# A two-layer block whose second expert layer handles 64 tokens by gathered rows and 192 densely

## The chip, the cores and the metric

The kernel runs on one core of one Trainium2 chip. The metric is the device time of one execution in microseconds (us). Engine names are those of the profile: PE is the matmul engine (TensorE), PEld its weight loads, DVE is VectorE, ACT is ScalarE, POOL is GpSimd, SP is SyncE, which issues most of the DMAs. L1385 is line 1385 of the kernel before.

## The reference

Two layers run over 256 latent tokens `x` and 256 context tokens `ctx`. In each layer a mixer (three kinds of sequence mixing, then an output projection) is followed by a product-key expert layer, `peer_ffn`, for every 128-token block. The change is in that expert layer for the last layer, where only the 256 latent tokens count:

```python
s = einsum('thpd,phkd->thpk', (xb @ w_query), keys)          # 8 heads, 2 halves, 128 keys each
...                                                          # the best 16 of 16*16 sums per head
idx, gate = ...                                              # 8*16 = 128 experts of 16384 for a token
act = gelu(einsum('td,thkd->thk', xb, expert_u[idx]))
out = einsum('thk,thkd->td', gate * act, expert_v[idx])      # expert_u, expert_v: [16384, 1024]
```

So each token uses 128 of the 16384 rows of `expert_u` and of `expert_v`. Everything is float32.

## The kernel before, in words

**Dense and gathered.** `peer` has two ways for a block of 128 tokens. The dense way multiplies the block by all 16384 experts and lets the gates, which are zero but at 128 places, pick. The gathered way fetches for each token (a partition) its own 128 rows of `expert_u` and 128 rows of `expert_v` with indirect DMAs from POOL's queue (`gather`, 128 rows of 4 KB in one DMA) and does the products on DVE: one SCALAR_TENSOR_TENSOR over 128x1024 for each u row (tile `grow`, L1277) and one for each v row (tile `gacc`, L1284). In layer 0 three blocks are dense and one is gathered (`gathered = {0: 0, 1: None}`). In layer 1 both blocks, 256 tokens, are dense.

**A dense expert step.** The 16384 experts go in 128 steps e of 128 experts. U(e) loads a tile of `expert_u` (512 KB, tile `eraw`), splits it into a rounded part `uhi` (ACT, L72) and the rest `ulo` (DVE, L73), multiplies both with the tokens' split `hTh`, `hTl` (the helper `mm3`: hi*hi, hi*lo and lo*hi for each of 8 chunks of the 1024 columns, 24 matmuls of 128 experts by 256 tokens in layer 1), and takes a gelu from PSUM (L1347). V(e) loads a tile of `expert_v`, splits it likewise into `vhi` and `vlo`, multiplies the step's activations by the gates (L1370), splits the product into the two halves of `whl` (L1372, L1373) and accumulates into PSUM (L1385): for each of two token blocks hi*hi, hi*lo and lo*hi over two halves of 512 columns, 12 matmuls of 512 columns. Each pair of split tiles has two buffers, `eraw` has five.

**The stages of layer 1.** After the queries and the top-k search, `gates` writes the dense gates out of one-hot products (L1225 to L1241, blocks of 8 tokens) to memory (`gd`), while U runs ahead for `LEAD[1]` = 56 steps. Of these activations some stay in SBUF and `SPILL[1]` = 14 go to memory and come back (tiles `aout`, `ain`). Then the main loop runs V(e), at first alone; from e = 52 on V(e) is followed by U(e+4). The gates come back in pieces for four steps (`gt`). At the end the residual, the norm and the output are done on DVE and ACT (L1458 to L1482).

**What sets the order.** The queue of each engine is in program order, fixed when the kernel is built by a scheduler with its own clock, so an instruction that waits holds up all behind it on its engine. `side()` puts pieces of the gathered way between the dense steps, `RATE` of them at each call; in layer 1 it has none to put.

## Time and profile before

| | us |
|---|---|
| median of 3 runs (2705.26 to 2716.01) | 2710.6 |
| the profiled execution's own time | 2711.68 |
| its span, first to last instruction | 2709.9 |
| layer 1: U alone beside the gates | about 1944 to 2122 |
| layer 1: V alone | 2122 to 2272 |
| layer 1: V and U in turn | 2272 to 2680 |
| the last V steps and the output | 2680 to 2710 |

The stages are read from the times of the first and last matmuls of each kind. PE is busy 96% of the span, DVE 75%. A busy PE here is one with a matmul in flight; matmuls overlap, so the time from the start of one to the start of the next, not the length of one, is what one costs.

### The profile page before, as it was taken

The numbers are of one execution on the slowest core, as the hardware profiler recorded it, in microseconds if no ns is written. First come the engines' busy times: TensorE is split into PE (matmuls) and PEld (weight loads), VectorE is DVE, ScalarE is ACT, GpSimd is POOL, SyncE is SP. The second block draws the span as 40 slices with busy tenths as digits, with TensorE's granted clock in tenths as the row PEclk, the third lists the DMA queues.
The fourth block names the chain that finished last, engine by engine and source line by source line (L and its number), as shares of the span: only waits on it lengthen the run. The fifth ranks groups of instructions, "written<-read, shape, count | busy, mean of one in ns | idle before, by whom it ended". The sixth has DMA issues, their size and how long they took to land.

```text
span 2709.9 us, 44308 instructions
## 1 busy us (share of the span) xinstructions
PE 2609.6 (96%) x16959; PEld 2264.6 (84%) x16959; DVE 2039.1 (75%) x4344; ACT 1187.5 (44%) x1808; POOL 415.2 (15%) x342
## 2 busy tenths in 40 slices
PE   7899999999899999999999999999899999999998
PEld 4677888898678899898899987868799878999997
DVE  8755589899789988888988855657999666555554
ACT  3343343466334333333333334444467545444443
POOL 0001000011014434344443300010010000000000
PEclk8998999999899999999999999989899999999999
DMA  7521523577679899999999938444577877666663
GB/s 275 129 92 56 176 90 109 192 286 293 224 253 361 316 347 327 344 337 334 326 340 339 339 113 266 136 142 178 175 262 265 280 236 244 209 209 209 208 209 115
DMA packets 253317, 632.77 MB, mean 234 GB/s; under 512 B 25840, under 2 KB 120880, under 8 KB 250288
## 3 DMA queue, kind: packets, MB, share of 16 engines
q1 hardware_dynamic: 198048, 433.19, 46.8%
q0 software_dynamic: 36864, 134.23, 13.7%
q10 hardware_dynamic: 18192, 62.50, 6.4%
q8 instruction: 133, 2.18, 0.3%
q14 instruction: 80, 0.66, 0.1%
HBM read 567.36 MB, written 61.45 MB: 232 GB/s over the span
## 4 chain that ended last, share of the span: by engine, by line
PE 78%; DVE 11%; issue 6%; DMA 3%; ACT 1%; POOL 0%; SPq 0%; DVEq 0%; POOLq 0%; ACTq 0%
PE pu L78 32%; PE acc L1385 28%; PE prT L280 5%; PE prN L294 3%; PE opp L947 2%; PE gps L1238 1%; PE gps L1239 1%; DVE wlo L73 1%; PE modp L158 1%; DMA ain<-act 1%; PE yp L639 1%; DVE ulo L73 1%; DMA mraw<-in_w_mod_dram 1%; DVE s L1096 1%; DVE ti L1095 1%
## 5 line engine op out<-in xcount | busy, mean ns | idle before, releaser
L1385 PE MATMUL acc<-vhi,whl 128*128 128x512 f32 x2528 | 726.2, 397 | 2.0 <-ACT whl L1372 2.0
L78 PE MATMUL pu<-hTh,uhi 128*128 128x384 f32 (+1 forms) x2048 | 605.2, 313 | 11.6 <-ACT s L1182 7.0
L78 PE MATMUL pu<-hTl,uhi 128*128 128x384 f32 (+1 forms) x2048 | 603.8, 313 | 0.0
L1385 PEld LDWEIGHTS acc<-vhi,whl 128*128 128x128 f32 x2528 | 471.4, 189 | 106.8 <-ACT whl L1372 2.3
L73 DVE TENSOR_TENSOR vlo<-eraw,vhi 128x1024 fp32r<-128x1024 f32 x253 | 309.2, 1222 | 261.7 <-ACT vhi L72 259.2
L72 ACT CAST vhi<-eraw 128x1024 fp32r<-128x1024 f32 x253 | 266.1, 1052 | 518.9 <-PE acc L1385 503.4
L1385 PE MATMUL acc<-vlo,whl 128*128 128x512 f32 x1264 | 402.2, 399 | 14.4 <-DVE vlo L73 14.4
L78 PEld LDWEIGHTS pu<-hTh,uhi 128*128 128x128 f32 x2048 | 391.6, 191 | 22.9 <-ACT s L1182 7.2
L78 PEld LDWEIGHTS pu<-hTl,uhi 128*128 128x128 f32 x2048 | 391.9, 191 | 6.8
L72 ACT CAST uhi<-eraw 128x1024 fp32r<-128x1024 f32 x259 | 272.3, 1052 | 269.7 <-PE pu L78 249.3
L73 DVE TENSOR_TENSOR ulo<-eraw,uhi 128x1024 fp32r<-128x1024 f32 x259 | 316.6, 1222 | 87.2 <-ACT uhi L72 66.1
L78 PE MATMUL pu<-hTh,ulo 128*128 128x384 f32 (+1 forms) x2048 | 352.5, 311 | 0.0
L78 PEld LDWEIGHTS pu<-hTh,ulo 128*128 128x128 f32 x2048 | 313.4, 190 | 3.1 <-DVE bsel L1154 0.8
L1385 PEld LDWEIGHTS acc<-vlo,whl 128*128 128x128 f32 x1264 | 238.4, 189 | 72.8 <-DVE vlo L73 16.6
L1271 POOL DMA_INDIRECT grow<-in_v_dram,gidx x128 | 167.9, 1311 | 253.7 <-DVE gacc L1284 196.4
L1271 POOL DMA_INDIRECT grow<-in_un_dram,gidx x128 | 154.5, 1207 | 279.1 <-DVE grow L1277 148.7
L73 DVE TENSOR_TENSOR wlo<-raw,whi 128x1024 fp32r<-128x1024 f32 x84 | 102.1, 1217 | 112.1 <-ACT whi L72 102.8
L1284 DVE SCALAR_TENSOR_TENSOR gacc<-grow,gact,gacc 128x1024 f32<-128x1024 f32 x127 | 162.6, 1280 | 3.0 <-DMA grow<-in_v_dram,gidx 3.0
L1277 DVE SCALAR_TENSOR_TENSOR grow<-grow,h2n 128x1024 f32<-128x1024 f32 x128 | 155.9, 1219 | 8.4 <-DMA grow<-in_un_dram,gidx 8.4
L280 PE MATMUL prT<-hTh,whi 128*128 128x512 f32 (+1 forms) x464 | 158.6, 347 | 2.9 <-ACT whi L72 2.9
L280 PE MATMUL prT<-hTl,whi 128*128 128x512 f32 (+1 forms) x464 | 159.6, 346 | 0.0
L280 PE MATMUL prT<-hTh,wlo 128*128 128x512 f32 (+1 forms) x464 | 157.5, 344 | 1.3 <-DVE wlo L73 1.3
(419 smaller groups left out, 3715.7 us busy)
## 6 DMA issues: line engine op xcount, KB each, us to landing
eraw<-in_ut_dram SPq DMA_DIRECT2D x256, 512.0 KB, 4.3
eraw<-in_v_dram SPq DMA_DIRECT2D x256, 512.0 KB, 4.5
gd<-gst ACTq DMA_DIRECT2D x20, 2048.0 KB, 8.5
mraw<-in_w_mod_dram SPq DMA_DIRECT2D x64, 512.0 KB, 4.8
gt<-gd SPq DMA_DIRECT2D x31, 768.0 KB, 10.4
raw<-in_w_in_dram SPq DMA_DIRECT2D x36, 512.0 KB, 5.0
raw<-in_w_query_dram SPq DMA_DIRECT2D x32, 512.0 KB, 3.8
eraw<-in_w_mod_dram SPq DMA_DIRECT2D x32, 512.0 KB, 6.3
```

The lines of the kernel that those rows point to most:

```text
L72: (hi_eng or nc.scalar.copy)(hi, src)
L73: self.last_lo = (lo_eng or nc.vector).tensor_tensor(lo, src, hi.bitcast(F32), op=OP.subtract)
L78: self.nc.tensor.matmul(out, a, b, start=n == 0, stop=n == len(ops) - 1)
L158: self.nc.tensor.matmul(acc[32 * kc:32 * kc + 32, :], self.sc[:, 4 * half + kc, :], raw[:, o:o + 512], start=half == 0 or not whole, stop= ...
L280: self.nc.tensor.matmul(bs[g][:, pt * n:pt * n + n], a[:, k, gs], b, start=z == 0 and k == 0 and q == 0, stop=z == 1 and k == 3 and q == 2)
L294: self.nc.tensor.matmul(o, a, b[:, k], start=z == 0 and k == 0 and q == 0, stop=z == 1 and k == 3 and q == 2)
L639: nc.tensor.matmul(bb[odd][:, gg, :], hin[hf, z, d, g // 2, :], rhs, start=n == 0, stop=False)
L947: mm = nc.tensor.matmul(ob[64 * k:64 * k + 64, cs], a, r, start=z == 0, stop=z == len(ops) - 1, tile_position=tp)
L1271: nc.gpsimd.indirect_dma_start(out=r, out_offset=None, in_=src, in_offset=bass.IndirectOffsetOnAxis(ap=idx[:, j:j + 1], axis=0))
L1277: v.scalar_tensor_tensor(r, r, 1.0, self.h2n, op0=OP.mult, op1=OP.mult, accum_out=act[:, j:j + 1])
L1284: v.scalar_tensor_tensor(acc, r, act[:, j:j + 1], acc, op0=OP.mult, op1=OP.add)
L1385: nc.tensor.matmul(acc[b][h], w[:, wk, bs], r[:, 512 * h:512 * h + 512], start=e_ == 0 and z == 0, stop=e_ == NI1 - 1 and z == 2)
```

## The change

In layer 1 the first 192 tokens stay dense and the last 64 (the second half of block 3) are gathered. So that the gathered half fills 128 partitions, each token takes two partitions with 64 of its 128 experts each: `h2n`, `gidx` and `ggate` hold tokens 64 to 127 of the block on the upper partitions and a copy for the other 64 experts on the lower ones. There are 64 u gathers and 64 v gathers of 512 KB each. `gates` makes 6 groups of 32 tokens, not 8.

U(e) keeps `hTh` and `hTl` in one tile `hTb`, so that one matmul of 384 columns multiplies `uhi` with both; a matmul of 192 columns multiplies `ulo` with the high part. That is 16 matmuls where there were 24. The two sums lie side by side in PSUM; ACT copies one, DVE adds the other (192 columns), ACT takes the gelu. V(e) writes the low and the high part of the last 64 tokens' activations side by side as one 128-wide stationary operand, so that block costs 4 matmuls of 512 columns and the other still 6: 10 where there were 12. At the end a matmul with a folding matrix adds the two halves of the gathered sums and of that block's PSUM.

`LEAD[1]` goes from 56 to 64, `SPILL[1]` from 14 to 32, and `RATE` for layer 1 is 1.0.

```diff
-LEAD = {0: 40, 1: 56}
+LEAD = {0: 40, 1: 64}
-SPILL = {0: 22, 1: 14}
+SPILL = {0: 22, 1: 32}
-RATE = 2.4
+RATE = {0: 2.4, 1: 1.0}
...
+    def split_tile(self):
+
+        self.hTb = self.hp.tile([128, 2, 8, 512], F32R, name="hTb", bufs=1)
+        return self.hTb[:, 0], self.hTb[:, 1]
...
+            if nat == self.half[l]:
+                nc.scalar.dma_start(self.h2n[0:64], self.h2n[64:128])
...
+        groups = [(b, tg) for b in blocks for tg in range(2 if b == self.half[l] else 4)]
...
+                    nc.vector.tensor_copy(self.gidx[hi], idx[hi, 0:64])
+                    nc.vector.tensor_copy(self.ggate[hi], w[hi, 2, 0:64])
+                    nc.scalar.dma_start(self.gidx[lo], idx[hi, 64:128])
+                    nc.scalar.dma_start(self.ggate[lo], w[hi, 2, 64:128])
...
+                    pu = pu_.tile([128, 2, nt], F32, name="pu", bufs=8 - 2 * nb)
+                    for c in range(8):
+                        cs = slice(c * 128, (c + 1) * 128)
+                        both = lambda: nc.tensor.matmul(pu, hi[:, cs], self.hTb[:, :, c, c0:c0 + nt],
+                                                        start=c == 0, stop=c == 7)
+                        if c < 7:
+                            both()
+                        nc.tensor.matmul(pu[:, 0], lo[:, cs], hs(hh, c), start=False, stop=False)
+                        if c == 7:
+                            both()
...
+                    nc.scalar.copy(acts[e], pu[:, 1])
+                    nc.vector.tensor_tensor(acts[e], acts[e], pu[:, 0], op=OP.add)
+                    nc.scalar.activation(acts[e], acts[e], AF.Gelu_apprx_tanh)
...
+                if half is not None:
+                    nc.scalar.copy(w[:, 2 * nt:], a[:, nt - nt % 128:])
...
-                for b in range(nb):
+                for b in range(nb) if half is None else (1, 0):
...
+                            if 128 * b + 128 > nt:
+
+                                ops = [(w[:, 2 * nt - 64:], r) for r in (hi, lo)]
+                            else:
+                                ops = [(w[:, o:o + 128], r) for o, r in ((128 * b, hi), (128 * b, lo), (nt + 128 * b, hi))]
...
+                    nc.tensor.matmul(b[0:64], fold, t, start=True, stop=True)
+                    nc.tensor.matmul(b[64:128], fold, self.gacc[:, 512 * h:512 * h + 512], start=True, stop=True,
+                                     tile_position=(0, 64))
...
             self.gathered = {0: 0, 1: None}
+            self.half = {0: None, 1: 3}
```

Line numbers in the rows of the changed program are its own (L1376 and L1380 are the two kinds of U matmuls, L1399 the addition, L1306 and L1313 the gathered products, L1423 and L1427 the gate product and the low half of `whl`).

PE in the main loop of layer 1, at the end of one U step and the start of the V step behind it, in the program before:

```order
L78 MATMUL pu<-hTh,uhi 128x256
L78 MATMUL pu<-hTl,uhi 128x256
L78 MATMUL pu<-hTh,ulo 128x256 x8
L1385 MATMUL acc_19974<-vhi,whl 128x512
L1385 MATMUL acc_19975<-vhi,whl 128x512
L1385 MATMUL acc_19974<-vlo,whl 128x512
L1385 MATMUL acc_19975<-vlo,whl 128x512
```

The same place in the changed program:

```order
L1376 MATMUL pu<-hTb,uhi 128x384
L1380 MATMUL pu<-hTb,ulo 128x192 x2
L1376 MATMUL pu<-hTb,uhi 128x384
L1445 MATMUL acc_19772<-vhi,whl 128x512
L1445 MATMUL acc_19773<-vhi,whl 128x512
L1445 MATMUL acc_19772<-vlo,whl 128x512
L1445 MATMUL acc_19773<-vlo,whl 128x512
L1445 MATMUL acc_19770<-vhi,whl 128x512
```

The `ulo` products, which stood in one run of 8 at the end of U, now alternate with the wide ones, and the second token block (`acc_19772`, `acc_19773`) has four matmuls and stands first.

DVE in the same loop, before (one U and two V steps in part):

```order
L73 TENSOR_TENSOR ulo<-eraw,uhi 128x1024
L1370 TENSOR_TENSOR act<-act,gt 128x256
L73 TENSOR_TENSOR vlo<-eraw,vhi 128x1024
L1373 TENSOR_TENSOR whl<-act,whl 128x256
L73 TENSOR_TENSOR ulo<-eraw,uhi 128x1024
```

DVE there in the changed program:

```order
L73 TENSOR_TENSOR vlo<-eraw,vhi 128x1024
L1306 SCALAR_TENSOR_TENSOR grow,gact<-grow,h2n 128x1024
L1313 SCALAR_TENSOR_TENSOR gacc<-grow,gact,gacc 128x1024
L1399 TENSOR_TENSOR act<-act,pu 128x192
L73 TENSOR_TENSOR ulo<-eraw,uhi 128x1024
L1423 TENSOR_TENSOR act<-act,gt 128x192
L73 TENSOR_TENSOR vlo<-eraw,vhi 128x1024
L1306 SCALAR_TENSOR_TENSOR grow,gact<-grow,h2n 128x1024
L1427 TENSOR_TENSOR whl<-act,whl 128x192
```

Gathered products stand between the splits of the dense steps, and each U brings an addition from PSUM.

DVE at the end of the gates of layer 1 (the one-hot products `oh1h`, `oh1l`), before:

```order
L1232 TENSOR_TENSOR oh1h<-oh1l,sel_18998 128x1024
L1233 TENSOR_TENSOR oh1l<-oh1l,sel_18998 128x1024
L73 TENSOR_TENSOR ulo<-eraw,uhi 128x1024
L1233 TENSOR_TENSOR oh1l<-oh1l,sel_18998 128x1024
L73 TENSOR_TENSOR ulo<-eraw,uhi 128x1024
L73 TENSOR_TENSOR vlo<-eraw,vhi 128x1024 x2
L73 TENSOR_TENSOR ulo<-eraw,uhi 128x1024
```

and in the changed program:

```order
L1252 TENSOR_TENSOR oh1h<-oh1l,sel_19032 128x1024
L73 TENSOR_TENSOR ulo<-eraw,uhi 128x1024
L1253 TENSOR_TENSOR oh1l<-oh1l,sel_19032 128x1024
L1399 TENSOR_TENSOR act<-act,pu 128x192
L73 TENSOR_TENSOR ulo<-eraw,uhi 128x1024
L1399 TENSOR_TENSOR act<-act,pu 128x192
L73 TENSOR_TENSOR ulo<-eraw,uhi 128x1024
L1399 TENSOR_TENSOR act<-act,pu 128x192
L1423 TENSOR_TENSOR act<-act,gt_19044 128x192 x2
```

After the last `oh1h`, 3 `ulo` splits stood before the main loop's run of V; now 16 do.

## Rows read from the trace of the kernel before

**Rows 1.** The page: span, then busy us (share of the span) xinstructions.
```profile
span 2709.9 us, 44308 instructions
PE 2609.6 (96%) x16959; PEld 2264.6 (84%) x16959; DVE 2039.1 (75%) x4344; ACT 1187.5 (44%) x1808; POOL 415.2 (15%) x342
```

**Rows 2.** Busy time by stage: us, each engine's busy us, PEclk, DMA share, GB/s.
```profile
core 0: us, PE busy (x) PEld busy (x) DVE busy (x) ACT busy (x) POOL busy (x), PEclk, DMA share, GB/s
1944.00:2122.00 178.00, 176.31 (x1686) 170.58 (x1687) 164.11 (x289) 121.06 (x188) 14.27 (x8) 0.99 0.72 258
2122.00:2272.00 150.00, 146.23 (x629) 117.21 (x628) 95.85 (x154) 69.96 (x105) 0.00 (x0) 0.99 0.75 251
2272.00:2680.00 408.00, 408.00 (x2577) 368.32 (x2577) 227.79 (x294) 195.57 (x290) 0.00 (x0) 1.00 0.62 209
```

**Rows 3.** Chain of waits, main loop of layer 1: start us, us, what.
```profile
2344.51 2.80 PE acc L1385 x12
2347.31 2.87 PE pu L78 x24
```

**Rows 4.** Waits of 1950 to 2710: us in total, times, longest us.
```profile
ACT vhi L72 <- PE acc L1385: 248.2, 122, 2.9
```

**Rows 5.** Timeline of PE, layer 0, one U step: start us, us, operation.
```profile
1243.38 0.33 PE L78 MATMUL pu<-hTh,uhi 128*128 128x384 f32 x1
...
1246.18 1.55 PE L78 MATMUL pu<-hTh,ulo 128*128 128x384 f32 x8
```

**Rows 6.** Timeline of PE, plain float32 matmuls, 128 and 512 columns.
```profile
1864.85 0.60 PE L1180 MATMUL sp<-keys,qTq 128*128 128x128 f32 x4
...
193.84 3.59 PE L664 MATMUL zp<-gyT,wglu 128*128 128x512 f32 x8
```

**Rows 7.** Timeline of DVE, layer 1, V alone.
```profile
2133.03 0.42 DVE L1373 TENSOR_TENSOR whl<-actr,whl 128x256 fp32r<-128x256 f32 x1
2133.37 0.42 DVE L1370 TENSOR_TENSOR actr<-actr,gt 128x256 f32<-128x256 f32 x1
```

**Rows 8.** Timeline of DVE, layer 0, with gathered products.
```profile
1357.72 1.22 DVE L1277 SCALAR_TENSOR_TENSOR grow<-grow,h2n 128x1024 f32<-128x1024 f32 x1
...
1358.87 1.28 DVE L1284 SCALAR_TENSOR_TENSOR gacc<-grow,gact,gacc 128x1024 f32<-128x1024 f32 x1
1360.07 1.22 DVE L73 TENSOR_TENSOR ulo<-eraw,uhi 128x1024 fp32r<-128x1024 f32 x1
1361.20 0.55 DVE L1370 TENSOR_TENSOR act<-act,gt 128x384 f32<-128x384 f32 x1
1361.67 0.42 DVE L364 TENSOR_TENSOR Rst<-rt 128x256 f32<-128x256 f32 x1
```

**Rows 9.** Busy time in two stretches of layer 0 that gather; columns of Rows 2.
```profile
820.00:870.00 50.00, 50.00 (x221) 40.97 (x220) 44.89 (x83) 20.12 (x27) 20.98 (x17) 1.00 1.05 383
1300.00:1400.00 100.00, 100.00 (x502) 90.24 (x501) 92.26 (x190) 36.50 (x48) 47.06 (x35) 1.00 0.97 342
```

**Rows 10.** Groups of DVE, 1944 to 2122: busy us, mean ns | idle.
```profile
L73 DVE TENSOR_TENSOR ulo<-eraw,uhi 128x1024 fp32r<-128x1024 f32 x47 | 57.5, 1223 | 9.5 <-ACT uhi L72 8.1 <-issue 1.1
L1232 DVE TENSOR_TENSOR oh1h<-oh1l,sel 128x1024 f16<-128x1024 f16 x32 | 22.0, 688 | 0.0
...
L1230 DVE TENSOR_SCALAR oh2s<-oh 128x1024 f16<-128x1024 f16 x16 | 6.7, 418 | 0.0
```

**Rows 11.** Groups of ACT, 2400 to 2500.
```profile
L72 ACT CAST uhi<-eraw 128x1024 fp32r<-128x1024 f32 x18 | 19.0, 1053 | 9.9 <-PE pu L78 9.9
...
L1347 ACT ACTIVATE act<-pu 128x256 f32<-128x256 f32 x18 | 6.9, 386 | 0.0
```

**Rows 12.** What ended idle time before the tile ain (us, times), whole run.
```profile
  DMA ain<-act: 16.5, 13
```

**Rows 13.** Busy time in 10 us among those waits; columns of Rows 2.
```profile
2180.00:2190.00 10.00, 8.62 (x30) 6.92 (x31) 6.90 (x11) 3.11 (x5) 0.00 (x0) 0.83 0.71 215
```

**Rows 14.** Timeline of DVE, the output behind the last matmul.
```profile
2696.87 1.89 DVE L1458 TENSOR_TENSOR et<-acc,gaterow 128x512 f32<-128x512 f32 x3 [5.09 <-PE acc L1385]
```

More of the change, by code (lines that the diff above doesn't have):

```diff
@@ L221, in norm_T @@
         s0 = 0 if which == 0 else 3
[L222 to L223 removed]
+        hT = self.split_tile()
         pairs = sorted({b // 2 for b in blocks})
@@ L1051, in mixer @@
             self.selp = self.es_sel.enter_context(self.pool(f"sel{l}", side="right"))
-            if self.gathered[l] is not None:
+            nat = self.gathered[l] if self.half[l] is None else self.half[l]
+            if nat is not None:
                 self.h2n = self.selp.tile([128, 1024], F32, name="h2n")
@@ L1080, in mixer @@
                 self.show("x1", xs[2])
-                self.norm_T(l, 1, xs, blocks, rp, nat=self.gathered[l], stats=ss, apart=blocks)
+                self.norm_T(l, 1, xs, blocks, rp, nat=nat, stats=ss, apart=blocks)
             self.tvp = self.es_tv.enter_context(self.pool(f"tv{l}", side="right"))
@@ L1210, in gates @@
         self.es_tv.close()
-        self.gt0 = es.enter_context(self.pool(f"gt0_{l}", side="right")).tile([128, 4 * len(blocks), HOLD[l], 32], F32, name="gt0")
+        self.gt0 = es.enter_context(self.pool(f"gt0_{l}", side="right")).tile([128, len(groups), HOLD[l], 32], F32, name="gt0")
         with self.pool(f"gate{l}", side="right") as p:
-            for k, b in enumerate(blocks):
+            for gi, (b, tg) in enumerate(groups):
                 sel = sels[b]
-                for tg in range(4):
+                if True:
                     st = p.tile([128, NI1, 32], F32, name="gst", bufs=2)
@@ L1284, in v_item @@
                 v.scalar_tensor_tensor(acc, r, act[:, j:j + 1], acc, op0=OP.mult, op1=OP.add)
-        for h in range(9):
+        for h in range(n // 16 + 1):
             for k in range(16):
-                if h < 8:
+                if h < n // 16:
                     u_item(16 * h + k)
@@ L1301, in peer @@
         nb = len(dense)
-        nt = 128 * nb
+        half = self.half[l]
+        nt = 128 * nb - (64 if half is not None else 0)
+        ng = nt // 32
         c0 = 128 * dense[0]
@@ L1312, in peer @@
             per, away = 1024 // nt, {}
+            kept = 4 * per if half is None else 8
+            held = lead - KEEP - spill - (kept if half is None else 0)
             pu_ = es.enter_context(self.pool(f"psu{l}", space=PSUM))
@@ L1332, in U @@
                 self.u_lo = self.last_lo
-                pu = pu_.tile([128, nt], F32, name="pu", bufs=8 - 2 * nb)
                 hs = lambda t, c: t[:, c, c0:c0 + nt]
-                self.mm3(pu, [((hi[:, c * 128:(c + 1) * 128], lo[:, c * 128:(c + 1) * 128]), (hs(hh, c), hs(hl, c)))
-                              for c in range(8)])
-                if e < 4 * per:
+                if half is None:
+                    pu = pu_.tile([128, nt], F32, name="pu", bufs=8 - 2 * nb)
+                    self.mm3(pu, [((hi[:, c * 128:(c + 1) * 128], lo[:, c * 128:(c + 1) * 128]), (hs(hh, c), hs(hl, c)))
+                                  for c in range(8)])
+                else:
[9 more added lines that the diff above has]
+                            both()
+                if e < kept and half is not None:
+                    acts[e] = acts_b.tile([128, nt], F32, name="act", bufs=held)
+                elif e < kept:
                     if e % per == 0:
@@ L1449, in peer @@
                 out[gb] = (self.gacc[:, 0:512], self.gacc[:, 512:1024])
-            for k, b in enumerate(sorted(out)):
+            if half is not None:
+                out[half] = []
+                fold = ep.tile([128, 64], F32, name="fold", bufs=1)
+                nc.vector.tensor_tensor(fold, self.ident[:, 0:64], self.ident[:, 64:128], op=OP.add)
+                for h in range(2):
+                    t = ep.tile([128, 512], F32, name="ft", bufs=2)
+                    nc.scalar.copy(t, acc[nb - 1][h])
+                    b = pubank([128, 512], "fold")
+                    nc.tensor.matmul(b[0:64], fold, t, start=True, stop=True)
+                    nc.tensor.matmul(b[64:128], fold, self.gacc[:, 512 * h:512 * h + 512], start=True, stop=True,
+                                     tile_position=(0, 64))
+                    out[half].append(b)
+            for k, b in enumerate(sorted(out) if half is None else (3, 2)):
                 ty = b // 2
```

62 lines of the change are left out of this document (38 added, 24 removed).

## The prediction, made before the changed kernel had run

> **What bounds the kernel now.** I read the page first: PE has a matmul in flight for 96% of the span, DVE works 75% [rows 1]. That share is a mean over stages, so next the busy times by stage of layer 1, the only part that the change touches. While U runs beside the gates, PE is busy 176 of 178 us and DVE 164; with V alone 146 of 150 against 96; with V and U in turn 408 of 408 against 228 [rows 2]. So in the last two stages, 558 us, PE sets the pace and DVE is idle two fifths of the time; in the first both are nearly full. The chain of waits agrees: in the main loop it is nothing but V of 12 matmuls for 2.80 us and U of 24 for 2.87 us by turns [rows 3], and the cast of `vhi` waits 248 us in all for PE to give its buffer back [rows 4]. The transfers run at 209 to 258 GB/s there [rows 2]. The change takes work from PE and gives work to DVE and the DMA engines, so the question is which of these two takes PE's place.
>
> **What PE saves.** A V of 10 matmuls costs 10/12 of 2.80 = 2.33 us. A U has 8 wide and 8 narrow ones. Wide: sixteen matmuls of 384 columns in layer 0 take 1246.18 - 1243.38 = 2.80 us, 0.175 each [rows 5]. Narrow (192 columns, this number type): no row. By columns it is 0.175/2 = 0.088. But each brings its own 128x128 weights; four plain float32 matmuls of 128 columns with such weights take 0.60 us, at most 0.15 each [rows 6], and 256 columns cost 2.87/24 = 0.12 now [rows 3]. I take 0.115, near the last, and keep 0.088 to 0.15. Then U = 8 x (0.175 + 0.115) = 2.32 us. PE saves 128 x 0.55 + 128 x 0.47 = 130 us in all.
>
> **What DVE gets.** Durations overlap by 0.08 us, so I use starts: 1.13 to 1.14 us for a split, 0.34 for 256 columns, 0.47 for 384 [rows 7, 8], hence 0.275 for 192. A gathered u product costs 1.15 us, a v product 1.20 [rows 8]. So V = 1.14 + 2 x 0.275 = 1.69 us and U, with its new addition, 1.415. That addition reads PSUM, which these rows do not show for this shape; 0.2 to 0.5 us holds it, and I take the SBUF price.
>
> The order of the built program cuts the loop in three. A: 64 V, 3 U and 60 gathered products (38 u, 22 v). B: 44 V, 45 U and 68 products (26 u, 42 v). C: the last 20 V and 16 U, with none.
> - A: PE 64 x 2.33 + 3 x 2.32 = 156 us. DVE 108.2 + 4.2 + 43.7 + 26.4 = 182 us.
> - B: PE 207 us. DVE 74.4 + 63.7 + 29.9 + 50.4 = 218 us.
> - C: PE 16 x 4.65 + 4 x 2.33 = 84 us, DVE 57.
>
> **What the DMA engines get.** A step's tile and a gather are 512 KB (0.524 MB) each, gates 0.39 MB for four steps, a spilled activation 0.1 MB. A moves 64 + 3 + 60 tiles, 14 gate pieces and 32 returning activations, 75 MB; B 44 + 45 + 68 tiles and 11 pieces, 87 MB. The best long stretch with gathers carried 383 GB/s, with PE never idle; a typical one 342, also with PE never idle, so 342 is a demand and not a limit [rows 9]. At 383 A takes 197 us and B 226, both a little over DVE and well over PE. So in A and B the feed decides, by transfers or by DVE, which lie within 15 us of each other. In A 32 activations come back from memory, where 14 did. Of 36 such tiles in the whole run 13 were waited for, 16.5 us in all [rows 12]: 32 x 13/36 x 1.27 = 15 us, of which I count half, since transfers go on meanwhile. A = 205, B = 229, C = 84: 518 us, against 2697 - 2122 = 575 now [rows 2, 14]. That is -57.
>
> At this place a page speaks against the change. The Trainium skill, DMA: Bandwidth & Descriptors, section Specifications, gives an HBM limit of about 358 GB/s for a core. By it A and B take 162/0.358 = 452 us instead of 434 and the sum ends 18 us later. Row and page differ: 383 over 50 us here, with one core at work.
>
> **Before the loop.** DVE comes to the last gate block earlier: 48 splits with an addition, 67.9 us, stand ahead of it instead of 53 without, 60.4; eight gate blocks fewer, each four one-hot operations of 0.61 and half of one of 0.34 (durations less the overlap of 0.08) [rows 10], 2.6 us, save 21; the extra rows and indices (`h2n`, `gidx`) cost some 3.5. Together -10 us. But 16 U steps stand behind that block where 3 stood, PE's 37.1 us instead of 8.6: +28.5. So V starts 18 us later, with 64 U done and not 56. Bounds -10 (PE finds room for them beside the gates) and +28.
>
> **Smaller edits.** ACT gets a PSUM copy in each U and a 64-column copy in each V, at most 0.39 us each beside casts of 1.05 [rows 11]; it is idle half of the main loop [rows 2], and that hides them; without that cover they would cost up to 0.8 us a step. Three small DMAs on ACT's queue and 18 more spills stand beside the gates, where transfers have room. On POOL four gathers stand ahead of the copies of the first gates, which wait for the last gate group anyway. On SP's queue the 32 returns stand among the loads of V; that wait is counted. One tile `hTb` for two means that a rewrite waits for readers of both; they end together, 0 to 2 us. Layer 0 keeps its work, some reordered: within 5 us. At the end two folds, four plain float32 matmuls of 512 columns at up to 0.45 us a record [rows 6], partly side by side, take the place of waiting for PE [rows 14]: +2.
>
> **The sum.** 2711.7 (the profiled execution's own time, 1.1 above the median of the runs) - 57 + 18 + 2 = 2675 us, or 2674 against the median. About 0.5% is what a measurement can tell from no change: 2697 to 2724.
>
> **Rivals.**
> - *All of PE's saving comes through.* 2711.7 - 130 = 2582. It needs A and B at PE's 363 us, but DVE alone has 400 there. Only a later, denser use of stage C could give it. 0.07.
> - *The feed is slower (the other side).* DVE's queue is in order: when a gathered row is late, the split behind it waits, and PE with it. If the mix of two queues yields R GB/s, A and B take 162/R. At 342, the typical row, the time is 2711.7 + 474 + 84 - 575 + 20 = 2715, no change; that is the point from which it decides (below 335 it is slower by over 0.5%). At 320 it is 2711.7 + 506 + 84 - 575 + 20 = 2747. For it: the small slack in A, where V's two buffers, casts and splits must fit in 2.33 us and a 1.2 us product may stand in between. Against it: 383 in a stretch where DVE did the same mix. Within 0.5% 0.10, slower 0.13.
> - *The clock falls in A.* Where V had waited for returning activations the granted clock was 0.83 over 10 us [rows 13], part of that at the lower level, 1.2 GHz; in steady V and U it was 1.00 [rows 2]. PE would be busy 156 of 205 us in A. At 1.2 GHz a V costs 10 x 512/1.2 = 4.27 us, A 275 us, the whole 2745. Against it: once PE is the slower one it is busy all the time, so this mends itself. Same 0.03, slower 0.04.
> - *The narrow matmuls run at the plain float32 price.* Such a matmul leaves two records of 3.59/8 = 0.45 us for 512 columns [rows 6], so 0.34 us for 192. U = 4.1 us, more than the 2.87 of now: the lead grows by 64 x 4.1 - 56 x 2.87 = 101 us (less some 6 of gate matmuls), B to 287, C to 112: 2711.7 + 95 + 605 - 575 + 2 = 2839. Against it: 256, 384 and 512 columns all cost 0.46 ns a column, with no sign of a step. 0.07.
> - *U does not get cheaper.* At 0.18 us for a narrow matmul U stays at 2.87 and only V saves; C costs 93 and the 16 late U steps 46, the time is 2675 + 9 + 9 + some 5 in B = 2698. Within 0.5% 0.04.
>
> **How the numbers follow.** The forecast, 2635 to 2697, has 0.52. Faster by over 0.5%: 0.52 + 0.07 = 0.59. Within: 0.10 + 0.03 + 0.04 = 0.17. Slower: 0.13 + 0.04 + 0.07 = 0.24. The range goes from 2625 (V starting early and the feed at PE's pace in half of A and B) to 2750 (a feed of 320); it leaves out the plain price, the full saving and some 0.05 of the slower feed, 0.19 in all.
>
> **What would show it.** In the changed profile: narrow matmuls 0.09 to 0.15 us apart; V at 3.1 to 3.3 us a step while alone and V with U at about 5.2 while gathers last; there PE busy about 80 to 90%, DVE over 90%, 370 to 390 GB/s; after the last gather 4.65 us a step with PE full; the first V near 2140 instead of 2122. I am wrong if DVE waits for `grow` by tens of us, if the granted clock in A is below 0.95, or if the stage before the first V is longer by more than 30 us.

## The result, and the profile after

The changed kernel takes 2684.5 us (median of 4 runs, 2681.19 to 2692.46) against 2712.4 (median of 4, 2705.26 to 2716.01): a ratio of 0.990, 95% interval 0.9886 to 0.9915, so 28 us or 1% faster, twice what a measurement can tell from no change. The prediction was 2674, range 2625 to 2750, with the forecast (faster, gathering stages set by the feed) as the likeliest case. The profiled execution took 2692.5, the slowest of its four, so single stages below may be some us long; that of before took 2711.7.

The page answers to [rows 1]: PE has 84 us less, DVE 146 us more.

```profile
span 2689.2 us, 42483 instructions
PE 2525.4 (94%) x15591; PEld 2141.6 (80%) x15591; DVE 2185.1 (81%) x4639; ACT 1217.7 (45%) x2054; POOL 593.8 (22%) x468
```

Busy time by stage, the columns of [rows 2]. The second to fourth rows are the prediction's A, B and C: they end where the low split of the 65th V, that of the 109th V and the last V matmul stand.

```profile
1944.00:2138.00 194.00, 168.01 (x1295) 151.13 (x1294) 171.34 (x355) 128.57 (x241) 19.66 (x10) 0.97 0.77 265
2138.00:2359.00 221.00, 186.34 (x751) 138.16 (x751) 190.68 (x306) 104.33 (x216) 88.25 (x61) 0.96 0.97 348
2359.00:2585.00 226.00, 210.93 (x1123) 177.78 (x1124) 216.76 (x312) 132.21 (x264) 101.17 (x63) 1.00 0.99 375
2585.00:2673.00 88.00, 88.00 (x493) 78.82 (x492) 59.74 (x89) 54.01 (x110) 0.00 (x0) 1.00 0.67 210
```

From first to last V matmul it is 535 us, where it was 572: -37. (The first V matmul of the kernel before stands at 2124.88 and the last at 2697.1; the 2122 and the 575 that the prediction used go by a boundary between stages.) The first V matmul stands 14 us later, the end behind the last V is 3 us longer. Together that makes the 20.7 us by which the span is shorter.

In B, 226 us, nothing is idle for long: the DMA engines are busy 0.99 of the time, DVE 217 us, PE 211. In C only PE is full. In A, 221 us, PE and DVE are each idle for over 30 us although the transfers, at 348 GB/s, are below B's 375. That stage is the odd one. Near its start the chain of waits (start us, us, what) names the tile that comes back from memory in two long pieces:

```profile
2166.56 6.66 DMA ain<-act
2185.05 9.47 DMA ain<-act
```

The DMA issues of the whole run (KB each, median us from issue to landing) show that such a tile takes longer: 5.6 us, where the larger one before took 3.9. First the changed kernel, then the one before:

```profile
ain<-act SPq DMA_DIRECT2D x32, 96.0 KB, 5.6
```

```profile
ain<-act SPq DMA_DIRECT2D x14, 128.0 KB, 3.9
```

DVE itself waited little for it (8.5 us in all, against 16.5 [rows 12]). The wait shows on ACT and PE instead: in the groups of 2165 to 2280, the PE matmuls of the first kind were held 22.9 us, most of it by the cast of `whl`, which stands behind the gate product on the returned tile.

```profile
L1445 PE MATMUL acc<-vhi,whl 128*128 128x512 f32 x191 | 63.3, 434 | 22.9 <-ACT whl L1426 19.6 <-DVE whl L1427 3.0 <-DVE gact L1326 0.2
L1426 ACT CAST whl<-ain 128x192 fp32r<-128x192 f32 x30 | 10.5, 349 | 22.8 <-DVE ain L1423 18.3 <-issue 4.5
L1423 DVE TENSOR_TENSOR ain<-ain,gt 128x192 f32<-128x192 f32 x29 | 9.9, 355 | 4.1 <-DMA ain<-act 4.1
```

But late tiles are not what makes this stage slow. Each gate product can be set beside the landing of the tile that it reads. For the 12th to the 19th V it starts within 0.5 us of the landing, so there the tile does come at the last moment; the low splits of these V go at 3.03 us a step. For the 20th to the 40th V the tile has landed 1.5 to 5.8 us before its product, and the steps from the 19th to the 41st take 3.77 us. These two stretches, in the columns of [rows 2]:

```profile
2173.60:2194.80 21.20, 16.24 (x65) 11.30 (x63) 18.42 (x32) 9.94 (x19) 9.78 (x6) 1.00 1.02 374
2200.20:2276.10 75.90, 58.26 (x207) 40.22 (x206) 58.63 (x92) 29.55 (x61) 24.72 (x20) 0.93 0.94 322
```

In the second, DVE never waits before the gate product (group of 2200 to 2276):

```profile
L1423 DVE TENSOR_TENSOR ain<-ain,gt 128x192 f32<-128x192 f32 x20 | 6.8, 354 | 0.0
```

What holds PE there is the order of the queues. In 18 of the 32 steps with a returned activation the gate product stands on DVE behind the same V's low split. In 12 of them, 11 behind the 19th V, the cast of `whl` also stands on ACT behind the cast of `vhi` for the next V, and its low half on DVE behind the next V's low split. The kernel before has none of either kind. `vhi` has two buffers, so the next V's cast waits until PE is through with the V before; PE then stands idle until both casts are done. At the start of the 34th V (timelines of PE and ACT, put in order of time; the engine's idle time before a row, and what ended it, in brackets):

```profile
2253.59 0.63 PE L1445 MATMUL acc<-vhi,whl 128*128 128x512 f32 x2
2254.30 1.04 ACT L72 CAST vhi<-eraw 128x1024 fp32r<-128x1024 f32 x1 [1.61 <-PE acc L1445]
2255.25 0.35 ACT L1426 CAST whl<-ain 128x192 fp32r<-128x192 f32 x1
2255.65 0.73 PE L1445 MATMUL acc<-vhi,whl 128*128 128x512 f32 x2 [1.43 <-ACT whl L1426]
```

PE's price is read in stage C (timeline of PE), in answer to [rows 3, 5]: U runs from 2600.13 to 2602.42, 2.29 us, V from there to 2604.75, 2.33 us. A wide and a narrow matmul together take 0.285 us: 0.18 to 0.20 to the next start behind a wide one, 0.085 to 0.09 behind a narrow one.

```profile
2600.13 0.34 PE L1376 MATMUL pu<-hTb,uhi 128*128 128x384 f32 x1
2600.31 0.25 PE L1380 MATMUL pu<-hTb,ulo 128*128 128x192 f32 x1
2600.40 0.36 PE L1376 MATMUL pu<-hTb,uhi 128*128 128x384 f32 x1
2600.60 0.25 PE L1380 MATMUL pu<-hTb,ulo 128*128 128x192 f32 x1
...
2602.42 0.63 PE L1445 MATMUL acc<-vhi,whl 128*128 128x512 f32 x2
...
2604.75 0.34 PE L1376 MATMUL pu<-hTb,uhi 128*128 128x384 f32 x1
```

DVE's prices in B (timeline of DVE), in answer to [rows 8]: the addition out of PSUM 0.26 us from start to start, a u product 1.15, a v product 1.19, the gate product 0.27.

```profile
2381.95 0.35 DVE L1399 TENSOR_TENSOR act<-act,pu 128x192 f32<-128x192 f32 x1
2382.21 1.22 DVE L1306 SCALAR_TENSOR_TENSOR grow<-grow,h2n 128x1024 f32<-128x1024 f32 x1
2383.36 0.08 DVE L1306 DVE_READ_ACCUMULATOR grow<-grow,h2n 128x1 f32 x1
2383.36 1.28 DVE L1313 SCALAR_TENSOR_TENSOR gacc<-grow,gact,gacc 128x1024 f32<-128x1024 f32 x1
2384.55 0.35 DVE L1423 TENSOR_TENSOR act<-act,gt 128x192 f32<-128x192 f32 x1
2384.82 1.22 DVE L73 TENSOR_TENSOR vlo<-eraw,vhi 128x1024 fp32r<-128x1024 f32 x1
```

Two questions remain: whether the feed in B is the transfers or DVE, and what holds A. All ratios below are to the kernel before, on the same chip; the changed kernel's is 0.990, and 0.001 is 2.7 us. Paces are from the start of one low split of V to that of the next, "V alone" those of the 9th to the 41st V (the ones with a returned activation), "V with U" those of the 61st to the 109th, "the steps behind" those of the 109th to the 125th.

### The profile page after: what moved, and what is told of

It reads as the page before. It is cut to its first block, busy times and chain, and to the rows that moved or that the text cites. A ratio compares the mean times of both kernels' runs of the same rounds, so it can differ in the third digit from the quotient of the medians.

```text
span 2689.2 us, 42483 instructions
## 1 busy us (share of the span) xinstructions
PE 2525.4 (94%) x15591; PEld 2141.6 (80%) x15591; DVE 2185.1 (81%) x4639; ACT 1217.7 (45%) x2054; POOL 593.8 (22%) x468
## 4 chain that ended last, share of the span: by engine, by line
PE 41%; issue 12%; DVE 10%; DMA 6%; ACT 4%; ACTq 0%; POOL 0%; SPq 0%; DVEq 0%; POOLq 0%
PE acc L1445 20%; PE pu L78 14%; PE pu L1376 2%; DMA act<-aout 2%; DVE ulo L73 2%; DVE vlo L73 2%; PE pu L1380 1%; ACT uhi L72 1%; DVE grow L1306 1%; DMA ain<-act 1%; ACT vhi L72 1%; PE prT L286 1%; DVE wlo L73 1%; DMA raw<-in_w_in_dram 1%; DVE gacc L1313 1%
## 5 line engine op out<-in xcount | busy, mean ns | idle before, releaser
L78 PE MATMUL pu<-hTb,uhi 128*128 128x384 f32 x2048 | 390.9, 341 | 7.7 <-ACT uhi L72 3.8
L1300 POOL DMA_INDIRECT grow<-in_un_dram,gidx x192 | 243.9, 1270 | 603.3 <-DVE grow L1306 198.6
L78 PEld LDWEIGHTS pu<-hTb,uhi 128*128 128x128 f32 x2048 | 362.2, 190 | 17.3 <-ACT actr L1396 4.7
L1300 POOL DMA_INDIRECT grow<-in_v_dram,gidx x192 | 271.2, 1412 | 347.1 <-DVE gacc L1313 215.9
L1376 PE MATMUL pu<-hTb,uhi 128*128 128x384 f32 x1024 | 320.7, 369 | 18.0 <-ACT uhi L72 16.0
L1380 PE MATMUL pu<-hTb,ulo 128*128 128x192 f32 x1024 | 250.2, 265 | 25.7 <-DVE ulo L73 24.8
L1313 DVE SCALAR_TENSOR_TENSOR gacc<-grow,gact,gacc 128x1024 f32<-128x1024 f32 x190 | 243.9, 1284 | 1.8 <-DMA grow<-in_v_dram,gidx 1.7
L286 PE MATMUL prT<-hTb,whi 128*128 128x512 f32 (+1 forms) x928 | 240.2, 346 | 3.5 <-ACT whi L72 3.2
L1306 DVE SCALAR_TENSOR_TENSOR grow<-grow,h2n 128x1024 f32<-128x1024 f32 x192 | 234.4, 1221 | 8.8 <-DMA grow<-in_un_dram,gidx 8.8
L1380 PEld LDWEIGHTS pu<-hTb,ulo 128*128 128x128 f32 x1024 | 198.6, 196 | 48.5 <-DVE ulo L73 41.4
L1376 PEld LDWEIGHTS pu<-hTb,uhi 128*128 128x128 f32 x1024 | 195.1, 193 | 27.6 <-ACT uhi L72 22.6
L78 PE MATMUL pu<-hTb,ulo 128*128 128x384 f32 x1024 | 204.0, 337 | 0.5 <-DVE ulo L73 0.5
L286 PEld LDWEIGHTS prT<-hTb,whi 128*128 128x128 f32 x928 | 159.8, 190 | 31.3 <-ACT whi L72 3.4
```

What stands on the lines that cost most here:

```text
L78: self.nc.tensor.matmul(out, a, b, start=n == 0, stop=n == len(ops) - 1)
L286: self.nc.tensor.matmul(bs[g][:, pt * n:pt * n + n], a[:, k, gs], b, start=z == 0 and k == 0 and q == 0, stop=z == 1 and k == 3 and q == 2)
L1300: nc.gpsimd.indirect_dma_start(out=r, out_offset=None, in_=src, in_offset=bass.IndirectOffsetOnAxis(ap=idx[:, j:j + 1], axis=0))
L1306: v.scalar_tensor_tensor(r, r, 1.0, self.h2n, op0=OP.mult, op1=OP.mult, accum_out=act[:, j:j + 1])
L1313: v.scalar_tensor_tensor(acc, r, act[:, j:j + 1], acc, op0=OP.mult, op1=OP.add)
L1376: both = lambda: nc.tensor.matmul(pu, hi[:, cs], self.hTb[:, :, c, c0:c0 + nt], start=c == 0, stop=c == 7)
```

## Experiments on the stages that gather

**No gathers.** Edit:

```diff
+        if n == 64:
+            v.memset(acc, 0.0)
+            return
         for h in range(n // 16 + 1):
```

> The 128 gathers and their 128 products on DVE are left out, so the last 64 tokens get no expert sum; all else is as in the changed kernel (2684 us). Theory F (in the stages that gather, the feed of transfers and DVE sets the pace): there V and U fall to PE's own 2.33 and 2.29 us, so about 2684 - (218 - 160) - (229 - 206) = 2600 us, and V alone takes 2.3 to 2.6 us a step. Rival A (the activations that come back from memory, tile ain, hold V while it is alone): V alone stays above 3.2 us a step and only the stage of V with U gains, 2655 to 2662. Rival C (PE's clock): the stretch of V alone still shows a granted clock under 0.95.

Measured 2616.8 us, ratio 0.9661 (0.9644 to 0.9678). V with U 4.51 us instead of 5.17, V alone 2.66 instead of 3.53, but 2.40 as soon as no activation comes back. Stages of 2160 to 2280 and of 2360 to 2560, columns of [rows 2]:

```profile
2160.00:2280.00 120.00, 112.38 (x471) 87.45 (x470) 83.70 (x141) 68.73 (x141) 0.00 (x0) 1.00 0.81 266
...
2360.00:2560.00 200.00, 200.00 (x1128) 180.38 (x1127) 145.08 (x218) 128.51 (x260) 0.00 (x0) 1.00 0.80 249
```

PE is full in the second stage and busy for 94% of the first, and the clock is 1.00 in both. So the gathers, transfers and products together, cost 65 us. The time fell short of the expected 2600: at this quick pace a return two steps ahead is late, and DVE waited 22.6 us for returned activations. None of the steps described above, with the cast of `whl` behind the next `vhi`, is in this kernel's order.

**A quarter of the products, and half of the bytes.** Edits, the first:

```diff
-            v.scalar_tensor_tensor(r, r, 1.0, self.h2n, op0=OP.mult, ...)
+            c = slice(0, 1024 if n == 128 else 256)
+            v.scalar_tensor_tensor(r[:, c], r[:, c], 1.0, self.h2n[:, c], op0=OP.mult, ...)
...
-                v.scalar_tensor_tensor(acc, r, act[:, j:j + 1], acc, ...)
+                v.scalar_tensor_tensor(acc[:, c], r[:, c], act[:, j:j + 1], acc[:, c], ...)
```

and the second, with the products reading `r[:, 0:512]` twice (`rep(r)`):

```diff
+            o = r
+            if n == 64:
+                o, src = r[:, 0:512], src.rearrange("a (b c) -> (a b) c", c=512)
-            nc.gpsimd.indirect_dma_start(out=r, out_offset=None, in_=src,
+            nc.gpsimd.indirect_dma_start(out=o, out_offset=None, in_=src,
```

> All rows are gathered, but each product on DVE covers 256 of the 1024 columns (part of the products is left out), so DVE has about 128 * 0.85 = 109 us less and the transfers are the same. If DVE's work sets the pace where V and U run by turns with gathers: 5.19 us a step falls to about 4.7 and the whole to 2640 to 2655. If the transfers set it: 5.1 to 5.2 us a step, 2675 to 2686.

> Each gather fetches 2 KB of a row where it was 4 KB (the first half of the columns is used twice), the products on DVE keep their 1024 columns: 34 MB less, DVE's work the same. If the transfers set the pace: 5.19 us a step falls to about 4.7, and V alone from 3.3 to 2.9, the whole to 2630 to 2655. If DVE's work sets it: 5.1 to 5.2 us a step, 2675 to 2686. If both kernels, this one and the one with quarter products, stay above 2670, the two limits lie on top of each other or the order of DVE's queue is it.

Measured: a quarter of the products 2682.8 us, ratio 0.9904 (0.9881 to 0.9927), no change; half of the bytes 2652.4, ratio 0.9787 (0.9765 to 0.9809), 31 us less. V with U keeps its 5.17 us a step with the small products and falls to 4.76 with the small transfers; V alone 3.70 and 3.04. The stage of 2360 to 2560 in the changed kernel,

```profile
2360.00:2560.00 200.00, 187.20 (x999) 157.79 (x999) 194.30 (x282) 115.99 (x233) 98.42 (x62) 1.00 1.01 382
```

with a quarter of the products,

```profile
2360.00:2560.00 200.00, 190.71 (x1018) 162.07 (x1016) 152.44 (x284) 118.11 (x239) 69.66 (x63) 0.99 1.02 389
```

and with half of the bytes:

```profile
2360.00:2560.00 200.00, 195.15 (x1082) 172.37 (x1081) 197.51 (x290) 125.16 (x254) 94.37 (x54) 1.00 0.92 318
```

DVE at 194 of 200 us looks full, and at 152 the steps are no faster; the DMA share of 1.01 to 1.02 at 382 to 389 GB/s is the limit. Take bytes away and DVE, at 197.5, is the next one, close behind. This holds for V with U, where none of the three kernels has a `whl` cast behind the next `vhi`. V alone is no clean test: of its 32 steps 12 have that order in the changed kernel, 17 with a quarter of the products and none with half of the bytes.

**Activations returned sooner.** Edit (`ain` moved to the pool that opens behind the gates, where there is room):

```diff
-                    acts[e] = p.tile([128, nt], F32, name="ain", bufs=AHEAD + 1)
+                    acts[e] = (p if half is None else p2).tile([128, nt], F32, name="ain", bufs=3 if half is None else 5)
...
-                back(e + AHEAD)
+                back(e + (AHEAD if half is None else 4))
```

> The returning activations are issued 4 steps ahead and not 2 (five ain buffers instead of three); nothing else changes. If their return is what makes V 8 to 39 slower (3.5 us a step against 3.1 before and after them): 2670 to 2676. If the feed of the whole stage holds it: 2680 to 2688.

Measured 2664.9 us, ratio 0.9842 (0.9825 to 0.986): 16 us less than the changed kernel and below the expected range. In the profiles V alone takes 2.99 us instead of 3.53 and stage A 197 us instead of 221. The three stages, as above:

```profile
2136.00:2333.00 197.00, 178.89 (x740) 131.59 (x740) 181.79 (x295) 104.05 (x212) 91.14 (x55) 0.99 1.01 371
2333.00:2560.00 227.00, 213.07 (x1145) 180.88 (x1144) 221.54 (x323) 135.26 (x270) 108.08 (x69) 1.00 1.02 386
2560.00:2647.00 87.00, 86.89 (x485) 77.48 (x485) 60.96 (x89) 53.15 (x107) 0.00 (x0) 1.00 0.66 222
```

A now has a DMA share of 1.01 like B, so the transfers' rate is the next limit there, and the granted clock, 0.96 in A before, is 0.99.

The edit changed more than its expectation says: the order that was fixed at the build is another one. No cast of `whl` stands behind the next `vhi` any more, and PE's wait for that cast over the 32 steps went from 18.3 us to 0. DVE waits for returned tiles no less than in the changed kernel, whose 4.1 us stand above (group of 2165 to 2250, nearly the same V):

```profile
L1423 DVE TENSOR_TENSOR ain<-ain,gt 128x192 f32<-128x192 f32 x28 | 9.9, 352 | 7.3 <-DMA ain<-act 7.2
```

From the 12th to the 19th V, where the tiles had come at the last moment, nothing was gained (3.13 us a step, 3.03 before). From the 19th to the 41st it went from 3.77 to 2.98, 17 us in all. The other kernels, those further down too, go with the order as well:

| kernel | steps of 32 with the `whl` cast behind the next `vhi` | PE's wait for the `whl` cast, us | V alone, us a step |
|---|---|---|---|
| the changed kernel | 12 | 18.3 | 3.53 |
| five `aout` buffers | 12 | 18.4 | 3.42 |
| U with 24 matmuls | 13 | 17.5 | 3.46 |
| V with 12 matmuls | 8 | 14.8 | 3.61 |
| a quarter of the products | 17 | 22.8 | 3.70 |
| rate of 0.7 | 9 | 14.7 | 3.10 |
| half of the bytes | 0 | 0.0 | 3.04 |
| returned sooner | 0 | 0.0 | 2.99 |
| no gathers | 0 | 0.4 | 2.66 |

The kernel with five `aout` buffers also has `ain` in the other pool, with the return still two steps ahead, so the move alone is not what helped. No run changed the order by itself, and why the scheduler chose it is not on record.

**Gathers spread over the whole loop.** Edit:

```diff
-RATE = {0: 2.4, 1: 1.0}
+RATE = {0: 2.4, 1: 0.7}
```

> RATE for layer 1 is 0.7 and not 1.0, so that the 128 gathers reach nearly to the last U step instead of ending 20 steps sooner; the same work. Transfer theory (380 to 389 GB/s is what the transfers can do, and they set the pace wherever there are gathers): 0.3 of the gathers of V alone, some 9 MB, and a few of V with U move to the last 20 steps, which now carry 226 GB/s: 12 to 25 us less, 2660 to 2672. If the returning activations alone hold V while it is alone, and not the gathers: 2676 to 2684. If the last gathers come too late and the output waits for them: above 2688.

Measured 2659.7 us, ratio 0.9813 (0.9792 to 0.9833), 24 us less, at the good end of what the transfer theory gave. V alone 3.10, V with U 4.97. The last product stands at 2619 instead of 2573, and the steps behind the 109th V, 4.46 us on average before, take 4.76. Stage C had held transfer time that nobody used: A takes 195 us, B 220 and C 90, 2 more. In A fewer gathers (21 products instead of 29 in the 32 steps) and a better order (9 steps instead of 12) come together and were not separated.

## Experiments on the two savings of PE, and on the stage before the loop

**V with 12 matmuls.** Edit (`zw` is a tile of zeros):

```diff
-                                ops = [(w[:, 2 * nt - 64:], r) for r in (hi, lo)]
+                                ops = [(w[:, 2 * nt - 64:], hi), (zw, lo), (w[:, 2 * nt - 64:], lo)]
```

> V with 12 matmuls of 512 columns again: the block with the side-by-side operand gets a third pair, with a stationary operand of zeros. Theory: the feed sets the pace where there are gathers, and there 2.80 us fit into 3.3 us (V alone) and 2.80 + 2.29 into 5.17; only the last 20 V steps pay, 20 * 0.47 = 9 us, and some of the denser steps: 2692 to 2704. If PE's saving on V comes through everywhere: 128 * 0.47 = 60 us more, 2735 to 2745.

Measured 2702.2 us (10 runs), ratio 0.997 (0.9959 to 0.998): 19 us more. In the profile the first 60 steps take 200.4 us against 198.6, V with U 5.22 against 5.17, the steps behind 4.95 against 4.46. Of the 60 us that V's two matmuls save on PE, 19 reach the time. The first 60 steps are no clean comparison, since only 8 of them, and not 12, have a `whl` cast behind the next `vhi`.

**U with 24 matmuls.** Edit:

```diff
-                        both = lambda: nc.tensor.matmul(pu, hi[:, cs], self.hTb[:, :, c, c0:c0 + nt], ...)
-                        ...
+                        nc.tensor.matmul(pu[:, 0], hi[:, cs], hs(hh, c), start=c == 0, stop=False)
+                        nc.tensor.matmul(pu[:, 0], hi[:, cs], hs(hl, c), start=False, stop=False)
+                        nc.tensor.matmul(pu[:, 0], lo[:, cs], hs(hh, c), start=False, stop=c == 7)
...
-                    nc.scalar.copy(acts[e], pu[:, 1])
-                    nc.vector.tensor_tensor(acts[e], acts[e], pu[:, 0], op=OP.add)
-                    nc.scalar.activation(acts[e], acts[e], AF.Gelu_apprx_tanh)
+                    nc.scalar.activation(acts[e], pu[:, 0], AF.Gelu_apprx_tanh)
```

> U without the side-by-side pass: three separate matmuls of 192 columns for each of the 8 chunks, 24 in all, into one sum; the ACT copy and the DVE addition fall away. The 576 columns of a chunk are the same. If a matmul costs by its columns (0.09 us for 192): U takes 2.1 to 2.2 us, the steps after the last gather 4.4 to 4.55 us, the whole 2672 to 2684, so that the side-by-side pass saves nothing. If a 192-column matmul with its own weights costs 0.115 as the prediction took: U 2.76 us, 5.1 us a step there, the whole 2695 to 2705.

Measured 2686.0 us, ratio 0.9914 (0.9892 to 0.9937): no difference from the changed kernel, and neither expectation whole. The timeline of PE in stage C:

```profile
2600.47 0.25 PE L1376 MATMUL pu<-hTb,uhi 128*128 128x192 f32 x1
2600.56 0.27 PE L1377 MATMUL pu<-hTb,uhi 128*128 128x192 f32 x1
2600.67 0.27 PE L1378 MATMUL pu<-hTb,ulo 128*128 128x192 f32 x1
2600.78 0.28 PE L1376 MATMUL pu<-hTb,uhi 128*128 128x192 f32 x1
...
2603.13 0.65 PE L1439 MATMUL acc<-vhi,whl 128*128 128x512 f32 x2
```

24 matmuls take 2.66 us, 0.111 each on average, so the side-by-side pass does save 0.37 us of PE a step, and stage C shows it (5.02 us from one U to the next against 4.62). But it costs a copy on ACT and an addition on DVE, and beside the gates, where those two are busy, the kernel without them has its first V matmul 14 us earlier, 2124.7 against 2138.5. The two about cancel. That the copy and the addition make all of the 14 us is not shown; leaving them out of the early U alone gave 4 us (below).

**More buffers for the activations that leave.** Edit (the room is that of `ain`, moved as above):

```diff
-                    acts[e] = p.tile([128, nt], F32, name="aout", bufs=2)
+                    acts[e] = p.tile([128, nt], F32, name="aout", bufs=2 if half is None else 5)
```

> Five aout buffers for the activations that leave for memory, where there were two; nothing else changes. The changed kernel's first V starts at 2138.5 us, 23.5 later than before, and ACT waits 23.3 us in all, 12 times, for an aout buffer. If these waits lengthen the stage before the first V: first V at 2120 to 2131, the whole 2666 to 2677. If the 16 U steps behind the last gate block do it: first V at 2136 to 2141, the whole 2680 to 2688.

The row it goes by, from the waits of 1950 to 2138 in the changed kernel (total us, times, longest):

```profile
ACT aout L1398 <- DMA act<-aout: 23.3, 12, 3.9
```

Measured 2678.6 us, ratio 0.9875 (0.9858 to 0.9892), 7 us less, with the first V matmul at 2130.6, 8 us earlier. That lies between the two expectations: about a third of the 23 us of waits was on the path; what keeps the rest was not separated. The intervals of this kernel and of the changed one overlap a little. The "23.5 later" of the expectation sets a matmul here against a split of the kernel before (2115.0); from first V matmul to first V matmul it is 13.6 us.

**All three together, and shorter leads.** The first kernel joins the earlier return, the five `aout` buffers and the rate of 0.7. The second has besides, for e below 48, the U with 24 matmuls and without the addition. The third and fourth differ from the second in:

```diff
-LEAD = {0: 40, 1: 64}
+LEAD = {0: 40, 1: 56}
-SPILL = {0: 22, 1: 32}
+SPILL = {0: 22, 1: 24}
```

and LEAD 48 with SPILL 16.

> Three edits together: activations return 4 steps ahead, five aout buffers, RATE 0.7. Transfer theory: single they gave 20, 6 and 25 us; the first and the third both relieve the stage of V alone, where the steps then fall to about 2.55 to 2.65 us, so they add up in part: first V at 2130, the whole 2636 to 2646. If one cause stood behind all three gains: 2656 to 2662.

> As the kernel with the three edits, and U(e) for e below 48, the steps beside the gates, with three separate matmuls of 192 columns for a chunk and no addition; the later U keep the side-by-side pass. With three matmuls everywhere the first V came at 2124.5 us instead of 2138.5, while U itself took 2.66 us against 2.29. If DVE and ACT hold the stage beside the gates: first V at 2112 to 2120, 8 to 18 us less than the kernel with the three edits. If it is the PE steps behind the last gate block alone: no gain from this, first V at 2128 or later.

> As the kernel with the three edits and the separate early U, with LEAD 56 and SPILL 24 as in the kernel before and in its proportion. The prediction charged 16 late U steps with 28 us of lead. If that holds, 8 late U steps less bring the first V forward by 15 to 19 us; the 8 U are then done among the V steps, at 2.29 us where PE is the limit or 1.4 us where the transfers are: the whole 1 to 8 us less than with LEAD 64. If the late U steps cost nothing: the first V moves by under 5 us and the whole is 5 to 15 us more.

> The same with LEAD 48 and SPILL 16, no late U step behind the gates. If the late steps are what they cost: first V 30 to 37 us earlier than with LEAD 64. The stage of V with U then has 80 steps, at PE's 4.65 or at the transfers' (0.524 * 2 + 0.1) / 0.385 = 3.0 us and 1.36 for each gather, 1.4 gathers a step, 4.9 us: the whole within 10 us of LEAD 56, on either side.

| kernel | us | ratio (95%) | first V matmul |
|---|---|---|---|
| three edits | 2648.2 | 0.9759 (0.9743 to 0.9775) | 2132.5 |
| and separate early U | 2646.2 | 0.9758 (0.9735 to 0.9781) | 2128.1 |
| and LEAD 56 | 2644.3 | 0.9745 (0.9729 to 0.9762) | 2117.0 |
| and LEAD 48 | 2646.2 | 0.9755 (0.9737 to 0.9773) | 2096.6 |

The three edits give 38 us where they give 16, 7 and 24 singly: they add up in most part, if a little less than expected (2636 to 2646), and the kernel is 2.4% faster than before. The four kernels of the table cannot be told apart. The separate early U brought 4 us of lead, not 8 to 18: the last one-hot product of the gates came 11 us earlier, but PE, which now has 2.66 us for each of 48 steps, did not follow. Its waits of 2000 to 2110 have at the top of ACT's list a wait for PE that the kernel with the three edits does not have among its longest:

```profile
ACT uhi L72 <- PE pu L1379: 19.8, 16, 3.2
```
 
With LEAD 56 the first V comes 11 us earlier than with 64, less than the expected 15 to 19. With LEAD 48 it comes 31 us earlier, as expected, and the time stays: the U steps that the lead no longer does are done in the loop. The stages of that kernel from the first V on:

```profile
2097.00:2330.00 233.00, 215.48 (x995) 172.47 (x994) 210.59 (x341) 127.45 (x263) 96.80 (x59) 0.98 0.99 363
2330.00:2560.00 230.00, 222.52 (x1205) 190.79 (x1204) 221.93 (x324) 137.69 (x279) 101.00 (x65) 1.00 1.01 379
2560.00:2629.00 69.00, 68.64 (x379) 60.20 (x377) 49.55 (x74) 41.97 (x85) 0.00 (x0) 1.00 0.65 228
```

In the middle stage PE has 222.5 of 230 us, DVE 221.9 and the DMA share is 1.01: three limits within 5% of each other. Which of them holds these kernels was not told apart.

## Why the prediction was right, point by point

**PE's saving.** V costs 2.33 us as worked out, U 2.29 for 2.32. The narrow matmul was put at 0.115; it is 0.09 behind a wide one and 0.111 in a row of its kind, and the wide one was 0.18 to 0.20 instead of 0.175, so the two errors cancelled in the sum. The plain float32 price, a rival of 0.07, is out, and so is a U that gets no cheaper.

**DVE.** In A to C DVE is busy 467 us (190.7 + 216.8 + 59.7) for 457 predicted. The addition out of PSUM, the one price without a row, is that of SBUF, 0.26 us for 0.275.

**The feed.** B was forecast at 226 us by transfers at 383 GB/s; the sum has 229 and gives no reason for the 3 us. By DVE's splits it took 226; by PE, which runs up to a step behind, 229 (the matmuls of the 65th V start at 2359.3, those of the 109th at 2588.6). That the transfers and not DVE set it could not be told from the trace of before, where the two lay 15 us apart; the quarter products and the half bytes settled it. The best stretch of [rows 9] was the right one to take: over 227 us the kernel with earlier returns carried 386. The Trainium skill, DMA: Bandwidth & Descriptors, section Specifications, has about 358 for a core. This trace, with one core at work, does not agree, by the 386. The 18 us that the prediction worked out from the page compare 452 us of transfers alone with 434 us that hold 11 us of other terms; like for like the estimate from the page would be 29. The prediction's sums for a slower feed leave out the same 11 us.

**Stage A is where the sum failed.** 205 us were forecast: 197 for the transfers and 8 for late returns (15 us, "of which I count half"). 221 came. The transfers' part is what remained in the kernel with the earlier return (197), and late returns are not where the sum was too small: DVE waited 8.5 us for them in the whole run. The term that it put at nothing, without a reason, is the order of the queues in A. There PE waited 18.3 us for casts of `whl`, which in 12 of the 32 steps stand behind the next `vhi`. The prediction read the order of the main loop and of the gates and not that of V alone; it named the tight place, "V's two buffers, casts and splits must fit in 2.33 us", only as an argument for the slower feed. An estimate: had the 22 steps from the 19th to the 41st V gone at the 3.03 us of the steps before them, A would have taken 221 - 22 x 0.74 = 205 us. That the order is the cause, and not late returns, rests on the landings and the waits in the traces; no run changed the order alone.

**C** was forecast at 84 us and took 88 from DVE's boundary, 85 from PE's: PE had fallen 3 us behind the splits when the last gathers ended.

**Before the loop.** +18 forecast, +14 measured. The last one-hot product of the gates stands at 2102.05 us, 9.6 earlier than before (2111.69), for a forecast of 10. From there to the first V matmul it is 36.5 us where it was 13.2: +23, for a forecast of +28.5. That the 36.5 lies near the 37.1 of 16 U is luck: 13 U stand in it, at 2.8 us each, and the other three come behind the first V, where the prediction's A counts them a second time. Timelines of DVE and of PE in the changed kernel, and of PE in the one before:

```profile
2102.05 0.70 DVE L1253 TENSOR_TENSOR oh1l<-oh1l,sel 128x1024 f16<-128x1024 f16 x1
```

```profile
2138.50 1.20 PE L1445 MATMUL acc<-vhi,whl 128*128 128x512 f32 x4 [1.49 <-ACT vhi L72]
```

```profile
2124.88 0.74 PE L1385 MATMUL acc<-vhi,whl 128*128 128x512 f32 x2 [0.77 <-ACT whl L1372]
```

Two things were missing in it all the same. The spills "where transfers have room" were not free: with two buffers ACT waited 23.3 us, and five buffers gave 7 us. And the term is no pure loss: U steps that leave the lead come back in the loop, as LEAD 48 showed.

**The end.** +2 forecast, +3 measured.

**The rivals.** All of PE's saving did not come through: at the measured prices PE saves 128 x (0.47 + 0.58) = 134 us; 28 arrived, and without gathers it is 92. The slower feed (342 GB/s over A and B as a limit) is out for B; A's 348 looked like it, but it was 374 while tiles came at the last moment and 322 later, while PE waited for casts. The granted clock of A was 0.96, above the 0.95 named as a sign of error, and 0.93 between 2180 and 2280, where PE stood idle again and again. It looks like a result of the waits and not a cause: with 12 matmuls for V, 20% more PE work, the first 60 steps took only 2 us more (if with 8 steps of the slow order and not 12), and with the earlier return the clock in A is 0.99.

```profile
2180.00:2280.00 100.00, 76.25 (x271) 52.78 (x270) 78.44 (x126) 40.00 (x82) 35.84 (x26) 0.93 0.95 336
```

**What would show it.** Measured: V with U 5.17 us a step for "about 5.2", C 4.62 for 4.65, first V at 2138.5 for "near 2140", 375 GB/s in B for 370 to 390. V alone at 3.53 where it has a returned activation is outside "3.1 to 3.3", and this is the sign that pointed to the failed step. PE in B was busy 93% for "80 to 90". DVE waited for `grow` 8.8 us before u products and 1.7 before v products in the whole run, not tens of us, and not at all in layer 1.

Of the 37 us that the sum promised against the profiled execution, 19 came; against the medians 28 of 36. The forecast was right in its cause for B and C and in its direction; that the total came so near owes something to errors that offset each other, as in the price of U.

## What to carry to other kernels

A change that takes work from the fullest engine and gives bytes to the DMA queues is worth what the transfers leave of it: divide the stage's bytes by the best rate that a long stretch of the same mix has shown, and compare that with the engines before counting a saving. When a load looks late, set its landing beside the start of the instruction that reads it: here the chain of waits named the returned tile, and for 21 of 32 steps it had landed 1.5 us or more before. Then read the order of every queue in the slow stage, not only in the main loop: an edit that moves a load can also move the casts, and a gain may come from that. A busy share of 97% does not make an engine the limit; taking its work away is a cheap test.
